# One slab of split weights converted at another place in the last attention head

## The chip, the cores and the metric

The kernel runs on one core of one Trainium2 chip. The metric is the device time of one execution in microseconds (us), the median of three runs.

The engines are named as in the profile: PE is TensorE (matmuls and transposes), DVE is VectorE, ACT is ScalarE, POOL is GpSimd, and SP is SyncE, which here only issues DMAs. Each engine works through its own instruction list in order, and an instruction waits until what it reads has been written and what it writes is free.

## The reference

The program is a diffusion backbone of two layers. Each layer projects the normed tokens (512 latent, 256 context) once, runs a convolution branch and an attention branch of eight heads on the result, merges them by gates and adds an MLP. Cut to what the change touches:

```python
for i in range(DEPTH):                                   # DEPTH = 2
    hx = modulate(rmsnorm(x, norm1_g[i]), sx1, ax1)
    px = hx @ w_in[i]                                    # [conv a | conv g | q | k | v | gates]
    q_x = apply_rope(rmsnorm(q_x, q_norm_g[i]), cos, sin)
    k_x = apply_rope(rmsnorm(k_x, k_norm_g[i]), cos, sin)
    keys = jnp.concatenate([k_x, k_c], axis=1)           # latent and context keys
    attn_x = diff_attention(q_x, keys, vals, lam, ...)   # two softmax maps a head
    # in merge_branches:
    a, g = u[..., :CONV_WIDTH], u[..., CONV_WIDTH:]      # CONV_WIDTH = 512
    z = a * jax.nn.sigmoid(g)                            # then a depthwise convolution of 31 taps
```

In the last layer the context tokens give only keys and values, no queries and no convolution.

## The kernel before

**Number format.** Every large product is computed from split fp32 operands: a high part `h`, a low part `l = x - h`, and three matmuls (lines 148 to 150): high by high, and each low part by the other's high part. A weight slab of 1024 x 256 (1 MB) is fetched by one DMA on SP's queue (line 107) into a tile with the tag `raw`, of which the attention stage has one, and then split in two halves of 128 x 1024: ACT copies the high part (`h_...`, line 76) and DVE subtracts for the low part (`l_...`, line 80). The next slab's DMA can start only when the low part of the second half is done, since it reads the raw tile. `load_slab` writes both steps; while `state["behind"]` holds instructions, the split is issued after them (`tc.issue_after`), the DMA is not.

**Attention.** Per head `h`, `qk_head(h)` projects each block of 128 tokens, norms and rotates it (ACT lines 804 and 807, DVE line 809, POOL lines 810 to 831, result `dup`) and turns it: four transposes on PE (`qkT`, line 842), a copy of the high part on ACT (line 846) and two subtractions on DVE (lines 847 and 849). `attend(h)` then makes, for each of the query blocks, the scores `S` (lines 978 and 980, two PSUM buffers), the reduction (DVE, line 982), the exponential `e` (ACT, line 985) and the difference of two softmax maps (DVE, line 995); it transposes the weights (`wT`, line 1008, into a single PSUM buffer), splits them into `wth` and `wtl` (lines 76 and 80) and multiplies them with the values (`av`). In names such as `wT0_6_1_1` the numbers are layer, head, block and half.

**Order.** A head's steps are written between those of the next head's `qk_head` (`merge`). While head 7 attends, the filling work is the projections for the convolution: `conv_a(0)`, `conv_a(1)` (blocks `ca`, slabs `wca..._0` and `wca..._1`), `conv_g(0)` and `conv_g(1)` (blocks `cg`, slabs `wcg`). Slab `a`,0 is loaded while head 7 is projected. The last two turns of head 7 are kept back (`late`) and put behind the first blocks of `conv_a(0)`: in layer 0 the two context blocks `qkT0_7_4` and `qkT0_7_5`, in layer 1 the last latent block `qkT1_7_3` and the context key (`kcD1_7`, whose norm runs over `kcT`, `rwc`, `sqe`, `rqk` and `dupc`, lines 866 to 891). `conv_a(s)` has two halves `m`; each makes a block of 512 latent tokens and, in layer 0, one of 256 context tokens. A scheduler then settles each engine's list from this program order and the waits.

**Behind.** In layer 1 DVE computes the taps of the convolution (`crun`, lines 1222 and 1226) while PE computes the merge gates (`gt`), and PE then needs their sum for a layer norm (`ln`, line 1332).

Before the change `conv_a` loads the next slab as soon as the first latent block of a slab is written, by the table `CONV_NEXT`; and `qk_head` notes a turned block in `turned` only in the last layer, at `t == 2`, so that the next head's slab is split behind it.

## Time and profile before

| | us |
|---|---|
| median of three runs | 2270.56 |
| lowest, highest | 2269.06, 2271.88 |
| profiled execution, its own time | 2273.66 |
| span of the profiled execution | 2271.9 |
| mean granted PE clock | 0.995 |

The page gives for one profiled execution the busy time of each engine in the span, and the chain of work that ended last. A row of the timeline has the start and the duration in us, the engine, the line, the instruction with its output and inputs (layer and block numbers left out), and in brackets the idle time of the engine ahead of it with what ended that. A row of the windows has the stretch, its length, the busy time (and number of instructions) of PE, of PE's weight loads, DVE, ACT and POOL, the granted clock of PE, the share of the DMA engines and GB/s.

### The profile page before, as it was taken

The numbers are of one execution on the slowest core, as the hardware profiler recorded it, in microseconds if no ns is written. First come the engines' busy times: TensorE is split into PE (matmuls) and PEld (weight loads), VectorE is DVE, ScalarE is ACT, GpSimd is POOL, SyncE is SP. The second block draws the span as 40 slices with busy tenths as digits, with TensorE's granted clock in tenths as the row PEclk, the third lists the DMA queues.
The fourth block names the chain that finished last, engine by engine and source line by source line (L and its number), as shares of the span: only waits on it lengthen the run. The fifth ranks groups of instructions, "written<-read, shape, count | busy, mean of one in ns | idle before, by whom it ended". The sixth has DMA issues, their size and how long they took to land.

```text
span 2271.9 us, 35812 instructions
## 1 busy us (share of the span) xinstructions
PE 2216.7 (98%) x14114; PEld 1999.1 (88%) x14114; DVE 1651.4 (73%) x2741; ACT 1046.9 (46%) x2035; POOL 630.9 (28%) x771
## 2 busy tenths in 40 slices
PE   7999999999999999999999999999999999999999
PEld 6999998888888999999999898999987788888887
DVE  5876777499767778788787557676759966757673
ACT  5555665432233264433445345565643333644541
POOL 1866775140000021111111345665623200000000
PEclk9999999999999999999999999999999999999999
DMA  9111102125354612332444522111114323443151
GB/s 308 57 47 47 48 27 67 45 98 169 128 174 141 203 50 65 105 121 84 139 140 144 168 75 59 45 36 52 45 61 150 115 93 121 149 135 105 57 185 38
DMA packets 202264, 232.59 MB, mean 102 GB/s; under 512 B 8864, under 2 KB 162928, under 8 KB 201968
## 3 DMA queue, kind: packets, MB, share of 16 engines
q1 hardware_dynamic: 202096, 230.30, 31.5%
q8 instruction: 111, 1.82, 0.3%
q14 instruction: 57, 0.47, 0.1%
HBM read 212.93 MB, written 17.35 MB: 101 GB/s over the span
## 4 chain that ended last, share of the span: by engine, by line
PE 75%; DVE 12%; ACT 4%; POOL 4%; DMA 3%; issue 2%; SPq 0%; DVEq 0%; POOLq 0%; ACTq 0%
PE r L157 5%; PE f L149 3%; PE f L148 3%; PE f L150 3%; PE r L148 3%; PE r L150 3%; PE r L149 3%; DVE crun L1226 3%; PE r L160 2%; PE qk L148 2%; PE qk L149 2%; PE qk L150 2%; PE gt L148 2%; PE gt L149 2%; PE gt L150 2%
## 5 line engine op out<-in xcount | busy, mean ns | idle before, releaser
L148 PE MATMUL qk<-h_wqk,h1h 128*128 128x256 f32 x640 | 182.7, 288 | 0.7 <-ACT h1h L76 0.7
L149 PE MATMUL qk<-l_wqk,h1h 128*128 128x256 f32 x640 | 180.2, 284 | 0.0
L982 DVE TENSOR_REDUCE st<-S 128x1 f32<-128x768 f32 (+1 forms) x160 | 134.4, 845 | 58.7 <-PE S L980 57.6
L150 PE MATMUL qk<-h_wqk,h1l 128*128 128x256 f32 x640 | 176.5, 284 | 0.0
L148 PE MATMUL f<-h2hh,h_w 128*128 128x512 f32 (+1 forms) x416 | 142.4, 345 | 1.5 <-ACT h2hh L76 1.4
L985 ACT ACTIVATE e<-S,st 128x768 f32<-128x768 f32 (+1 forms) x160 | 130.8, 820 | 27.9 <-DVE st L982 27.8
L149 PE MATMUL f<-h2hl,h_w 128*128 128x512 f32 (+1 forms) x416 | 143.1, 346 | 0.0
L150 PE MATMUL f<-h2hh,l_w 128*128 128x512 f32 (+1 forms) x416 | 142.5, 344 | 0.0
L148 PE MATMUL gt<-h1h,h_wg 128*128 128x512 f32 (+1 forms) x384 | 137.9, 359 | 1.0 <-ACT g L1308 1.0
L150 PE MATMUL gt<-h1h,l_wg 128*128 128x512 f32 (+1 forms) x384 | 136.1, 355 | 0.0
L149 PE MATMUL gt<-h1l,h_wg 128*128 128x512 f32 (+1 forms) x384 | 136.1, 354 | 0.0
L148 PEld LDWEIGHTS qk<-h_wqk,h1h 128*128 128x128 f32 x640 | 122.2, 191 | 3.1 <-ACT h1h L76 0.9
L157 PE MATMUL r<-F,wlor 128*128 128x512 f32 (+1 forms) x384 | 124.2, 339 | 0.4 <-DVE wlor L1639 0.4
L157 PE MATMUL r<-F,whir 128*128 128x512 f32 (+1 forms) x384 | 123.5, 337 | 0.2 <-ACT F L1582 0.2
L149 PEld LDWEIGHTS qk<-l_wqk,h1h 128*128 128x128 f32 x640 | 122.2, 191 | 0.0
L330 DVE SCALAR_TENSOR_TENSOR adaac<-ar,cvec,adaac 128x512 f32<-128x512 f32 x105 | 94.9, 926 | 35.8 <-DMA ar<-in_w_ada_dram 34.0
L150 PEld LDWEIGHTS qk<-h_wqk,h1l 128*128 128x128 f32 x640 | 119.9, 191 | 0.3 <-POOL h1l L80 0.2
L1226 DVE SCALAR_TENSOR_TENSOR cacc<-z,cols,cacc 128x783 f32<-128x783 f32 x120 | 118.8, 1045 | 0.0
L148 PE MATMUL v<-h_wv,h1h 128*128 128x256 f32 x384 | 112.3, 293 | 5.6 <-DVE qk L849 3.5
L149 PE MATMUL v<-l_wv,h1h 128*128 128x256 f32 x384 | 109.5, 285 | 0.0
L150 PE MATMUL v<-h_wv,h1l 128*128 128x256 f32 x384 | 109.4, 285 | 0.0
L810 POOL TENSOR_TENSOR rqk<-rqk,mhalf 128x4 f32<-128x4 f32 x80 | 85.8, 1075 | 76.0 <-DVE rqk L809 74.6
(406 smaller groups left out, 7392.7 us busy)
## 6 DMA issues: line engine op xcount, KB each, us to landing
r_w<-in_w_mlp_dram SPq DMA_DIRECT2D x34, 1024.0 KB, 5.3
ada<-in_w_ada_dram SPq DMA_DIRECT2D x24, 1024.0 KB, 5.3
ar<-in_w_ada_dram SPq DMA_DIRECT2D x96, 256.0 KB, 3.3
r_wg<-in_w_in_dram SPq DMA_DIRECT2D x16, 1024.0 KB, 5.4
r_wqk<-in_w_in_dram SPq DMA_DIRECT2D x30, 512.0 KB, 5.2
rf<-in_w_mlp_dram SPq DMA_DIRECT2D x26, 512.0 KB, 3.9
rr<-in_w_mlp_dram SPq DMA_DIRECT2D x24, 512.0 KB, 3.7
r_wao<-in_w_attn_out_dram SPq DMA_DIRECT2D x8, 1024.0 KB, 5.2
```

What stands on the lines that cost most here:

```text
L148: nc.tensor.matmul(ps, sh, mh, start=first, stop=False)
L149: nc.tensor.matmul(ps, sh, ml, start=False, stop=False)
L150: nc.tensor.matmul(ps, sl, mh, start=False, stop=last)
L157: nc.tensor.matmul(ps, w[j][:, k, m0 : m0 + P], a(k)[0][:, toks], start=k + j == 0, stop=False)
L160: nc.tensor.matmul(ps, w[0][:, k, m0 : m0 + P], a(k)[1][:, toks], start=False, stop=k == nk - 1)
L330: nc.vector.scalar_tensor_tensor(out=a, in0=r, scalar=cvec[:, k, q : q + 1], in1=a, op0=ALU.mult, op1=ALU.add)
L810: nc.gpsimd.tensor_tensor(out=r, in0=r, in1=mhalf[:, :4], op=ALU.pow)
L982: nc.vector.tensor_reduce(out=st[:, m : m + 1], in_=S[:, :nkey], axis=AX.X, op=ALU.max, negate=True)
L985: nc.scalar.activation(out=e[:, :nkey], in_=S[:, :nkey], func=AF.Exp, bias=st[:, m : m + 1], accum_out=st[:, 2 + m : 3 + m])
L1226: nc.vector.scalar_tensor_tensor(out=(run if t < TAPS - 1 else ca[cc])[:, :CV], in0=zt[cc][:, t : t + CV], scalar=wcol, in1=run[:, :CV], o ...
```

## The change

The slab `a`,1 is loaded in `conv_a(0)` after the second latent block, `(s, m) == (0, 1)`, in place of the first, and its split is issued behind the copies of the last head's last turned block. For that, `turned[h]` is now also set for the last head, in both layers and at every block, so that it holds the last block that is turned by then: `qkT0_7_5` in layer 0, `qkT1_7_3` in layer 1. The slab `g`,0 is loaded at the place where it was, and the table goes. No instruction is added or taken away on any engine.

```diff
-        CONV_NEXT = {("a", 0): ("a", 1), ("a", 1): ("g", 0), ("g", 0): ("g", 1)}
...
-                    if m == 0 and g is LAT:
-                        conv_w[CONV_NEXT["a", s]] = conv_load(*CONV_NEXT["a", s])
+                    if (s, m) == (1, 0) and g is LAT:
+                        conv_w["g", 0] = conv_load("g", 0)
+                    if (s, m) == (0, 1) and g is LAT:
+                        state["behind"] = turned[H - 1]
+                        conv_w["a", 1] = conv_load("a", 1)
+                        state["behind"] = ()
                     yield 5.3 if g is LAT else 2.7
...
-                if last and t == 2:
+                if last and t == 2 or h == H - 1:
                     turned[h] = hi.ins, lo.ins
```

How the engines' lists change. Behind line 740 the changed kernel's line numbers are higher by 3, so line 846 is 849 there, and 985 is 988. ACT in layer 0, from the last projection of head 7 on (`rw0_7_5`), before:

```order
L804 ACTIVATE rw0_7_5_5347<-qk0_7_5_5322 128x256
L76 ACTIVATE h_wca0_1_5444<-r_wca0_1_5442 128x1024 x2
L846 ACTIVATE qk0_7_4860<-qkT0_7_3_5361 128x4x128
L807 ACTIVATE sqe0_1_708<-rw0_7_5_5347 128x4x64
L76 ACTIVATE wth0_6_0_0_4824<-wT0_6_1_0_4991 128x3x128
L846 ACTIVATE qk0_7_4860<-qkT0_7_4_5369 128x4x128
L985 ACTIVATE e10_6_3_5168,st0_6_3_5153<-S0_6_3_1_5162,st0_6_3_5153 128x768
```

And the changed kernel on ACT, from the split of a transposed block of head 6 on, a few rows later in the list:

```order
L1026 ACTIVATE osq0_6_0_5096<-av0_6_0_5077 128x256
L1028 ACTIVATE uo0_6_0_5098<-av0_6_0_5077,ag0_141 128x256
L76 ACTIVATE wth0_6_1_0_5050<-wT0_6_2_0_5175 128x3x128
L849 ACTIVATE qk0_7_4860<-qkT0_7_5_5377 128x4x128
L76 ACTIVATE h_wca0_1_5535<-r_wca0_1_5533 128x1024 x2
L988 ACTIVATE e10_6_4_5255,st0_6_4_5244<-S0_6_4_1_5251,st0_6_4_5244 128x256
L1041 ACTIVATE rsall0_711<-av0_6_0_5077,es20_6_0_4828 128x1 x2
L76 ACTIVATE wth0_6_1_1_5052<-wT0_6_2_1_5181 128x3x128
```

The two copies `h_wca0_1` have moved from ahead of the copy of `qkT0_7_3` to behind that of `qkT0_7_5`. DVE's two subtractions `l_wca0_1` move likewise, from between two score reductions to behind its copies of `qkT0_7_5`. On SP the load of `r_wca0_1` keeps its place; `r_wcg0_0`, which needs the raw tile, moves behind the two loads of `gr` and the write of `uo0_6_0`.

ACT in layer 1, from the first copy of the slab to the copy of the last turned block, before:

```order
L76 ACTIVATE h_wca1_1_18387<-r_wca1_1_18385 128x1024
L985 ACTIVATE e11_6_3_18264,st1_6_3_18249<-S1_6_3_1_18258,st1_6_3_18249 128x768
L76 ACTIVATE h_wca1_1_18387<-r_wca1_1_18385 128x1024
L846 ACTIVATE qk1_7_17909<-qkT1_7_2_18283 128x4x128
L76 ACTIVATE wth1_6_0_1_17875<-wT1_6_1_1_18105 128x3x128
L985 ACTIVATE e01_6_3_18256,st1_6_3_18249<-S1_6_3_0_18250,st1_6_3_18249 128x768
L860 ACTIVATE kc1_7_18247<-kc1_7_18222 128x256
L868 ACTIVATE rwc1_7_18306<-kcT1_7_18303 128x256
L871 ACTIVATE sqe1_1_14387<-rwc1_7_18306 128x4x64
L846 ACTIVATE qk1_7_17909<-qkT1_7_3_18314 128x4x128
```

And the changed kernel on ACT, from the context key's copy `rwc1_7` on:

```order
L871 ACTIVATE rwc1_7_18306<-kcT1_7_18303 128x256
L849 ACTIVATE qk1_7_17909<-qkT1_7_3_18314 128x4x128
L76 ACTIVATE h_wca1_1_18442<-r_wca1_1_18440 128x1024 x2
L874 ACTIVATE sqe1_1_14387<-rwc1_7_18306 128x4x64
L1041 ACTIVATE rsall1_14390<-av1_6_0_18185,es21_6_0_17877 128x1 x2
L76 ACTIVATE wth1_6_1_1_18113<-wT1_6_2_1_18277 128x3x128
L76 ACTIVATE wth1_6_1_0_18111<-wT1_6_3_0_18291 128x3x128
L76 ACTIVATE wth1_6_1_1_18113<-wT1_6_3_1_18297 128x3x128
L894 ACTIVATE qk1_7_17909<-kcD1_7_18322 128x2x256
```

The two copies now stand behind that of `qkT1_7_3` and ahead of the context key's square `sqe1_1` and of the split `wth1_6_1_1`. On DVE the two subtractions `l_wca1_1` likewise stand behind the copies of `qkT1_7_3` and ahead of `rqk` (line 873) and `wtl1_6_1_1`.

PE in layer 1, from the transposes of a softmax block to the first block of the convolution, before:

```order
L1008 MATMUL wT1_6_2_0_18271<-cst_75,e01_6_2_18123 128x128 x3
L978 MATMUL S1_7_0_0_18335<-qk1_7_17909 128x512
L980 MATMUL S1_7_0_0_18335<-qk1_7_17909 128x512
L978 MATMUL S1_7_0_1_18343<-qk1_7_17909 128x512
L980 MATMUL S1_7_0_1_18343<-qk1_7_17909 128x512
L1034 MATMUL av1_6_0_18185<-cst_75,osq1_6_0_18204 128x1 x2
L1008 MATMUL wT1_6_2_1_18277<-cst_75,e01_6_2_18123 128x128 x3
L887 MATMUL kcD1_7_18322<-cst_75,dupc1_7_18312 128x128 x4
L148 MATMUL ca1_0_0_18359<-h1h_1_13449,h_wca1_0_18042 128x512
```

And the changed kernel on PE, from the same transposes on:

```order
L1011 MATMUL wT1_6_2_0_18271<-cst_75,e01_6_2_18123 128x128 x3
L869 MATMUL kcT1_7_18303<-cst_75,kc1_7_18247 128x128 x2
L845 MATMUL qkT1_7_3_18314<-cst_75,dup1_7_3_18177 128x128 x4
L1037 MATMUL av1_6_0_18185<-cst_75,osq1_6_0_18204 128x1 x2
L1011 MATMUL wT1_6_2_1_18277<-cst_75,e01_6_2_18123 128x128 x3
L981 MATMUL S1_7_0_0_18335<-qk1_7_17909 128x512
L983 MATMUL S1_7_0_0_18335<-qk1_7_17909 128x512
L981 MATMUL S1_7_0_1_18343<-qk1_7_17909 128x512
L983 MATMUL S1_7_0_1_18343<-qk1_7_17909 128x512
L1011 MATMUL wT1_6_3_0_18291<-cst_75,e01_6_3_18256 128x128 x3
L148 MATMUL av1_6_1_18385<-wth1_6_1_0_18111,vh1_3_17200 128x256
L1011 MATMUL wT1_6_3_1_18297<-cst_75,e01_6_3_18256 128x128 x3
```

In the list of before the transposes `wT1_6_3_0` come after 23 matmuls of `ca1_0_0`; now they stand ahead of `ca1_0_0`, with `wT1_6_3_1` and nine matmuls of `av1_6_1`. The later transposes of head 7 move forward too: `wT1_7_1_1` stood after eight matmuls of `cg1_2_0` and now stands after eight of `cg1_1_0`; `wT1_7_3_0` and `wT1_7_3_1`, which had one matmul between them, now have 33 of the merge gates and that one.

## The prediction

> **What bounds the kernel now.** I read the page first: busy shares and the chain that ended last by engine.

> ```profile
> PE 2216.7 (98%) x14114; PEld 1999.1 (88%) x14114; DVE 1651.4 (73%) x2741; ACT 1046.9 (46%) x2035; POOL 630.9 (28%) x771
> ...
> PE 75%; DVE 12%; ACT 4%; POOL 4%; DMA 3%; issue 2%; SPq 0%; DVEq 0%; POOLq 0%; ACTq 0%
> ```

> TensorE (PE) is busy for 98% of the span, so the change can only touch PE's few waits, stretches in which PE's clock is halved, and the DVE piece of the chain. Next I read the timeline of PE around both places where the second `a` slab is converted. Layer 0 (start, duration, instruction, idle time before it and what ended that):

> ```profile
> 381.73 0.44 PE L842 MATMUL qkT<-cst,dup 128*128 128x128 f32 x2 [0.20 <-POOL dup L831]
> 383.42 0.44 PE L842 MATMUL qkT<-cst,dup 128*128 128x128 f32 x2 [1.25 <-POOL dup L831]
> ...
> 385.42 0.58 PE L978 MATMUL S<-qk 128*128 128x256 f32 x1 [1.45 <-ACT e L985]
> ...
> 386.65 0.90 PE L1008 MATMUL wT<-cst,e 128*128 128x128 f32 x3 [0.43 <-DVE wtl L80]
> ...
> 390.12 0.63 PE L149 MATMUL ca<-h1l,h_wca 128*128 128x512 f32 x1
> 390.55 0.60 PE L150 MATMUL ca<-h1h,l_wca 128*128 128x512 f32 x1
> ...
> 402.48 0.50 PE L148 MATMUL ca<-h1h,h_wca 128*128 128x512 f32 x1 [0.36 <-ACT z L737]
> ...
> 415.04 0.40 PE L148 MATMUL ca<-h1h,h_wca 128*128 128x512 f32 x1
> 415.28 0.40 PE L149 MATMUL ca<-h1l,h_wca 128*128 128x512 f32 x1
> ...
> 375.00:390.00 15.00, 11.66 (x74) 10.54 (x73) 13.71 (x25) 9.74 (x20) 11.37 (x16) 0.81 0.22 70
> ```

> The waits sum to 0.20 + 1.25 + 1.45 + 0.43 + 0.36 = 3.69 us. The `ca` matmuls of 512 columns start 0.43 us apart at 390.12 but 0.24 apart at 415.04, and the granted clock of the stretch (the figure 0.81, after the busy times) is below 1: the clock is halved. A mean of 0.81 over 15 us is 0.19 x 15 / 0.5 = 5.7 us at half speed. Layer 1:

> ```profile
> 1645.34 0.52 PE L1008 MATMUL wT<-cst,e 128*128 128x128 f32 x3 [0.35 <-DVE wtl L80]
> ...
> 1648.16 0.38 PE L148 MATMUL av<-wth,vh 128*128 128x256 f32 x1 [1.34 <-ACT wth L76]
> 1649.95 0.41 PE L866 MATMUL kcT<-cst,kc 128*128 128x128 f32 x2 [1.41 <-DVE qk L849]
> 1650.89 1.11 PE L842 MATMUL qkT<-cst,dup 128*128 128x128 f32 x4 [0.54 <-DVE wtl L80]
> ...
> 1650.00:1660.00 10.00, 9.42 (x48) 8.28 (x49) 5.43 (x11) 3.98 (x10) 4.24 (x6) 0.83 0.37 120
> ```

> Here the waits sum to 3.64 us, and 0.17 x 10 / 0.5 = 3.4 us run at half speed.

> **Layer 0: what goes.** The conversions and what they hold up:

> ```profile
> 379.72 2.00 ACT L76 ACTIVATE h_wca<-r_wca 128x1024 fp32r<-128x1024 f32 x2
> ...
> 381.56 1.21 DVE L80 TENSOR_TENSOR l_wca<-r_wca,h_wca 128x1024 fp32r<-128x1024 f32 x1
> ...
> 380.94 2.42 POOL L831 TENSOR_TENSOR dup<-rw,gr 128x256 f32<-128x256 f32 x2
> 387.89 1.42 POOL L831 TENSOR_TENSOR dup<-rw,gr 128x256 f32<-128x256 f32 x2
> ```

> ACT spends 2.00 us on the high parts ahead of the copy of the head's fourth block; DVE spends 2 x 1.21 on the low parts between two score reductions; and POOL's pair that makes `dup` takes 2.42 us beside a DVE subtraction, 1.42 without. With the conversions gone from here, POOL's second half is ready 1.0 us earlier, and the exponential that frees the scores' buffer is not behind 2.0 us of ACT and 1.2 of DVE. Replaying PE's new order with these durations leaves 0.2 (first transposes), 0.6 (second), 0.5 (`wT0_6_1_1`) and 0.4 (scores, and `qkT0_7_5` behind them), and I add 0.3 for what the replay misses: 2.0 us for 3.69, a **gain of 1.7**.

> The clock: from 385.42 to 391 PE works 5.13 us (5.56 less the wait of 0.43) at 0.43 us a matmul for 0.24. Full clock saves 5.13 x (1 - 0.24/0.43) = 2.3; with 0.23, which most neighbouring starts show, 2.4. I take **2.4**. No row shows how few idle us keep the clock up. In the 3.4 us ahead of the drop PE was idle for 1.25 + some 0.5 of the next wait, about 1.75; my replay's worst stretch of that length has 1.3. So I take the clock as full, bounds 0 to 2.4. [...]

> What takes the conversions' place is later: they stand behind the copies of `qkT0_7_5`, about 390 to 394 us. Their slab is first read by `ca0_2_0`, which starts at 415.04: 20 us of cover. The raw buffer is single, so the next load moves:

> ```profile
> 384.80 0.38 SPq L107 DMA_DIRECT2D r_wcg<-in_w_in_dram  x1
> ...
> r_wg<-in_w_in_dram SPq DMA_DIRECT2D x16, 1024.0 KB, 5.4
> ...
> 415.37 1.08 ACT L76 ACTIVATE h_wcg<-r_wcg 128x1024 fp32r<-128x1024 f32 x1
> ```

> It is issued at about 394 in place of 384.80, behind two 32 KB loads and one output write on SP's queue, lands 5.4 us later (an equal slab) at 399.4, and is read at 415.37, or 411 if all is 4 us earlier: 11 us of cover. Cost 0; without that cover each us late would be one. Layer 0: **4.1**, bounds 1.7 to 4.4.

> **Layer 1: what comes.** Here the conversions move behind the copies of `qkT1_7_3` and thereby ahead of the context key's norm and of `wtl1_6_1_1`, for which PE's transposes `wT1_6_3_0` wait:

> ```profile
> 1646.19 1.05 ACT L76 ACTIVATE h_wca<-r_wca 128x1024 fp32r<-128x1024 f32 x1
> ...
> 1650.81 0.42 ACT L871 ACTIVATE sqe<-rwc 128x256 f32<-128x256 f32 x1
> ...
> 1656.11 0.49 ACT L76 ACTIVATE wth<-wT 128x384 fp32r<-128x384 f32 x1 [0.18 <-PE wT L1008]
> ...
> 1652.00 0.42 DVE L873 TENSOR_REDUCE rqk<-sqe 128x4 f32<-128x260 f32 x1
> 1652.68 0.43 DVE L847 TENSOR_TENSOR qk<-qkT,qk 128x256 fp32r<-128x256 f32 x1 [0.26 <-ACT qk L846]
> ...
> 1654.91 0.56 DVE L80 TENSOR_TENSOR wtl<-wT,wth 128x384 fp32r<-128x384 f32 x1 [0.91 <-ACT wth L76]
> ...
> 1645.93 1.20 POOL L811 TENSOR_TENSOR rw<-rw,rqk 128x256 f32<-128x256 f32 x1
> ...
> 1647.90 1.84 POOL L823 TENSOR_TENSOR rb<-rw,tS 128x128 f32<-128x128 f32 x2
> ...
> 1652.50 1.04 POOL L874 TENSOR_TENSOR rqk<-rqk,mhalf 128x4 f32<-128x4 f32 x1 [1.20 <-DVE rqk L873]
> ```

> Count from E, the end of ACT's copy of `qkT1_7_3`. DVE's two copies take 2 x 0.43, then the scores start (E + 0.9) and last 1.0. ACT's first half ends at E + 1.05; DVE's two subtractions of 1.21 end at E + 3.5, then `rqk` 0.42 and `wtl` 0.56: E + 4.5. PE, ready at E + 1.9, waits 2.6, less 0.3 in which its pipeline drains (the trace counts that as busy): **2.3**. POOL's `rqk` of 1.04, DVE's product of 0.4 and the next `wtl` keep the last pair `wT1_6_3_1` waiting for 0.9 more. Ahead of E: 0.35 as now; 0.2 for `av`; 1.1 for `dup` (POOL's chain, with about 0.6 and 0.9 saved in the two rows above where the subtractions no longer run beside it); 1.1 for the scores (transposes, 0.6 + 0.43 + 0.43, less the work between). Sum 6.0 for 3.64: PE is **2.3 later**. The half-clock stretch cost about 3.4 x 0.45 = 1.5; with waits that are longer than before I expect it again, so it cancels; bounds: gone, or twice.

> How much of this reaches the end is read behind it:

> ```profile
> 1702.48 1.52 DVE L1222 TENSOR_SCALAR crun<-z,cols 128x512 f32<-128x512 f32 x2
> ...
> 1710.00:1720.00 10.00, 10.00 (x49) 8.31 (x48) 10.00 (x16) 3.18 (x6) 1.87 (x1) 1.00 0.01 4
> ...
> 1724.86 0.38 PE L148 MATMUL av<-wth,vh 128*128 128x256 f32 x1 [0.58 <-ACT wth L76]
> 1725.79 0.55 PE L1008 MATMUL wT<-cst,e 128*128 128x128 f32 x3 [0.55 <-DVE wtl L80]
> ...
> 1812.76 1.12 PE L1332 MATMUL ln<-tot,cst 128*128 128x512 f32 x2 [2.71 <-DVE tot L1329]
> ```

> From 1702.48 on DVE runs the convolution's taps without a pause (10.00 of 10.00), and at 1812.76 PE waits 2.71 us for the last of them. So PE has 2.71 us in hand there, and the taps decide. In the new order PE does the last head's softmax transposes earlier among the convolution's gate blocks: `wT1_7_1_1` comes 24 matmuls of `cg` sooner, and DVE's first tap, queued behind the splits of those transposes, moves from 1702.48 to between 1699 and 1701. The same shift puts 22 matmuls of the merge gates (22 x 0.23 = 5 us) between `wT1_7_3_0` and its first reader, so the waits of 0.58 and 0.55 go: 1.1. PE reaches the norm 2.3 - 1.1 = 1.2 later, waits 2.71 - 1.2 = 1.5 less, and the taps, 1.5 to 3.5 earlier, allow it. Layer 1: a **gain of 1.5**, bounds -1.1 (second half-clock stretch, tail not shorter: 2.71 - 2.3 - 1.5) and +2.7 (the whole wait goes).

> **Sum.** 4.1 + 1.5 = 5.6 us. The profiled execution took 2273.66 us, so 2268.1; it stands 3.1 above the median of the runs (2270.56), so **2265.0** by the median.

> **Rivals.**
> - *Clock full in layer 1 too.* Then PE is 1.5 less late, the wait at the norm goes whole: 4.1 + 2.7 = 6.8, 2263.8. For it: a drop needs a stretch idle enough, and before only one followed. Against: 2.3 us is the longest wait of both kernels. [...]
> - *Clock still halved in layer 0* for one stretch of 3.4 us: it costs 1.5 of the 2.4. 5.6 - 1.5 = 4.1, 2266.5. For it: 1.3 idle us in a stretch is not far from 1.75.
> - *Layer 1 takes all of its part back*: the tail's waits stay and the taps start no earlier, 2.71 - 2.3 = 0.4, or down to -1.1: 4.1 - 0.35 = 3.75, 2266.8. For it: DVE's order is fixed and a later PE can hold its first tap.
> - *Slower.* The new waits behind `h_wca1_1` throw the clock to half and keep it there. Half speed costs about 0.45 us for each busy us, so the 5.6 are gone after 12.4 us (3.6 stretches) more than I assume; with four, 13.6 us, 6.1 us go: 2271.1. Slower by over 0.2% needs 10.1 / 0.45 = 22 us. Against: the longest run of halved clock here is two stretches.
> - *The load is not asked for later.* In the order of SP's queue `r_wca0_1` keeps its place between the same two output writes; only conversions move. That changes no term above.

> **How the numbers follow.** Forecast 0.38, clock full in layer 1 0.15, halved in layer 0 0.19, layer 1 takes it back 0.19, slower or something the replay misses 0.09. 0.2% of 2270.56 is 4.5 us, about what a measurement of this kernel can tell from no change. Below 2266.0: most of the forecast (0.34), all of the first rival, little of the next two (0.04): 0.53. Slower by over 0.2%: 0.06, from the last. The rest, 0.41, is within. The range: 2262.0, which is the best sum with both bounds (4.4 + 2.7 = 7.1, 2263.5) less 1.4, half the spread of the three runs (2269.06 to 2271.88); up to 2271.2, which takes in the slower rival's price.

> **What would show it.** Right: no half-speed stretch between 380 and 395 us, waits of about 2 us there, `ca0_1_0` near 398.4 for 402.48; in layer 1 one wait of over 2 us at transposes for `wtl`, the first tap at about 1700 less the gain of layer 0, and a shorter wait at `ln`. Wrong: PE idle before `cg0_0_0` for its weights, a granted clock under 0.9 in layer 0's stretch, or a wait at `ln` of 2.7 again.

## The result and the profile after

| | before | changed |
|---|---|---|
| median of 12 runs, us | 2272.39 | 2268.61 |
| lowest, highest | 2268.24, 2277.10 | 2265.84, 2271.69 |
| profiled execution, its own time | 2273.66 | 2268.69 |
| span of the profiled execution | 2271.9 | 2266.9 |

The ratio of the changed kernel to the one before is 0.998, 95% interval 0.9972 to 0.9987: 4.5 us (3.0 to 6.4) for a forecast of 5.6. In another set of 11 runs (e11 below) it was 0.9975 (0.9967 to 0.9984). The page of the changed kernel, busy time and chain:

```profile
PE 2218.0 (98%) x14114; PEld 2000.4 (88%) x14114; DVE 1652.4 (73%) x2741; ACT 1047.1 (46%) x2035; POOL 627.3 (28%) x771
...
PE 74%; DVE 12%; DMA 4%; ACT 4%; POOL 3%; issue 2%; SPq 0%; DVEq 0%; POOLq 0%; ACTq 0%
```

The page hardly changes: 5 us of 2270 are looked for in the timeline. The changed kernel's PE in layer 0, then POOL, ACT, DVE and SP at the same place, and the windows' row for the stretch:

```profile
380.69 0.44 PE L845 MATMUL qkT<-cst,dup 128*128 128x128 f32 x2 [0.21 <-POOL dup L834]
...
382.48 0.55 PE L1011 MATMUL wT<-cst,e 128*128 128x128 f32 x3 [0.66 <-DVE wtl L80]
...
384.49 0.38 PE L981 MATMUL S<-qk 128*128 128x256 f32 x1 [0.40 <-ACT e L988]
...
397.06 0.50 PE L148 MATMUL ca<-h1h,h_wca 128*128 128x512 f32 x1
...
379.90 1.42 POOL L834 TENSOR_TENSOR dup<-rw,gr 128x256 f32<-128x256 f32 x2
...
390.01 2.00 ACT L76 ACTIVATE h_wca<-r_wca 128x1024 fp32r<-128x1024 f32 x2
...
410.06 2.03 ACT L76 ACTIVATE h_wcg<-r_wcg 128x1024 fp32r<-128x1024 f32 x2
...
391.10 2.36 DVE L80 TENSOR_TENSOR l_wca<-r_wca,h_wca 128x1024 fp32r<-128x1024 f32 x2
...
393.49 0.38 SPq L107 DMA_DIRECT2D r_wcg<-in_w_in_dram  x1
...
375.00:390.00 15.00, 13.60 (x93) 11.99 (x92) 11.80 (x25) 9.37 (x22) 9.15 (x15) 1.00 0.05 14
```

Three waits are left, 1.27 us for 3.69, and the granted clock is 1.00 for 0.81. From the first transposes of `qkT0_7_4` to `ca0_1_0` it is 397.06 - 380.69 = 16.37 us, for 402.48 - 381.73 = 20.75. The conversions run from 390.01, and the load behind them, issued at 393.49, is read at 410.06; nothing waits for either. Layer 1, PE's waits, the conversions and the windows' row:

```profile
1640.39 0.52 PE L1011 MATMUL wT<-cst,e 128*128 128x128 f32 x3 [0.35 <-DVE wtl L80]
1642.56 0.39 PE L149 MATMUL av<-wtl,vh 128*128 128x256 f32 x1 [0.58 <-DVE wtl L80]
1645.02 0.65 PE L845 MATMUL qkT<-cst,dup 128*128 128x128 f32 x4 [0.69 <-POOL dup L831]
1647.35 0.47 PE L981 MATMUL S<-qk 128*128 128x512 f32 x1 [0.95 <-ACT h_wca L76]
1650.62 0.90 PE L1011 MATMUL wT<-cst,e 128*128 128x128 f32 x3 [2.11 <-DVE wtl L80]
1652.11 0.58 PE L148 MATMUL av<-wth,vh 128*128 128x256 f32 x1 [0.58 <-ACT wth L76]
...
1646.20 2.00 ACT L76 ACTIVATE h_wca<-r_wca 128x1024 fp32r<-128x1024 f32 x2
...
1647.29 2.36 DVE L80 TENSOR_TENSOR l_wca<-r_wca,h_wca 128x1024 fp32r<-128x1024 f32 x2
...
1640.00:1660.00 20.00, 14.72 (x77) 12.15 (x77) 10.56 (x19) 9.06 (x21) 8.62 (x11) 0.83 0.18 60
```

The waits sum to 5.26 us for 3.64; the longest, 2.11 us, is for the split `wtl1_6_1_1` behind the conversions. The clock's 0.83 over 20 us is 0.17 x 20 / 0.5 = 6.8 us at half speed (0.50 from 1649.51 to 1656.33), for 3.4 before. Behind it, the first tap, PE's waits up to the layer norm, and then the first matmul of the layer's output projection in the kernel before (first row) and in the changed one (second):

```profile
1694.72 0.81 DVE L1225 TENSOR_SCALAR crun<-z,cols 128x512 f32<-128x512 f32 x1
...
1725.87 0.61 PE L1037 MATMUL av<-cst,osq 128*128 128x1 f32 x4 [0.90 <-ACT uo L1028]
...
1759.63 0.50 PE L148 MATMUL gt<-h1h,h_wg 128*128 128x512 f32 x1 [0.24 <-ACT g L1311]
...
1798.76 0.47 PE L148 MATMUL ya<-h1h,h_wao 128*128 128x512 f32 x1 [0.76 <-ACT g L1311]
...
1805.69 1.12 PE L1335 MATMUL ln<-tot,cst 128*128 128x512 f32 x2 [0.77 <-DVE tot L1332]
```

```profile
1879.90 0.39 PE L148 MATMUL o<-mh,h_wo 128*128 128x512 f32 x1
```

```profile
1873.74 0.39 PE L148 MATMUL o<-mh,h_wo 128*128 128x512 f32 x1
```

From the first row of layer 1 (1645.34 before) to this one it is 234.56 us before and 233.35 after. So by the traces layer 0 gains 4.4 us and layer 1 1.2. The rest of the span differs between two profiles by some us either way (from that `o` to the last matmul 387.6 us before and 388.8 after; there the clock of the changed kernel was at 0.50 from 1925.99 to 1929.40 us, that of before at 1.00 throughout).

### The profile page after: what moved, and what is told of

Same layout as the page of the kernel before. It is cut to its first block, busy times and chain, and to the rows that moved or that the text cites. A ratio compares the mean times of both kernels' runs of the same rounds, so it can differ in the third digit from the quotient of the medians.

```text
span 2266.9 us, 35816 instructions
## 1 busy us (share of the span) xinstructions
PE 2218.0 (98%) x14114; PEld 2000.4 (88%) x14114; DVE 1652.4 (73%) x2741; ACT 1047.1 (46%) x2035; POOL 627.3 (28%) x771
## 4 chain that ended last, share of the span: by engine, by line
PE 74%; DVE 12%; DMA 4%; ACT 4%; POOL 3%; issue 2%; SPq 0%; DVEq 0%; POOLq 0%; ACTq 0%
PE r L157 4%; PE f L149 4%; PE f L150 4%; PE f L148 3%; PE r L148 3%; PE r L149 3%; PE r L150 3%; PE qk L148 3%; DMA ar<-in_w_ada_dram 2%; PE qk L149 2%; PE qk L150 2%; DVE crun L1229 2%; PE gt L148 2%; PE gt L149 2%; PE gt L150 2%
## 5 line engine op out<-in xcount | busy, mean ns | idle before, releaser
L148 PE MATMUL qk<-h_wqk,h1h 128*128 128x256 f32 x640 | 182.6, 287 | 0.7 <-ACT h1h L76 0.7
L149 PE MATMUL qk<-l_wqk,h1h 128*128 128x256 f32 x640 | 180.2, 284 | 0.0
L985 DVE TENSOR_REDUCE st<-S 128x1 f32<-128x768 f32 (+1 forms) x160 | 134.4, 846 | 59.3 <-PE S L983 58.3
L150 PE MATMUL qk<-h_wqk,h1l 128*128 128x256 f32 x640 | 176.5, 284 | 0.0
L148 PE MATMUL f<-h2hh,h_w 128*128 128x512 f32 (+1 forms) x416 | 142.9, 347 | 1.5 <-ACT h2hh L76 1.4
L149 PE MATMUL f<-h2hl,h_w 128*128 128x512 f32 (+1 forms) x416 | 143.9, 347 | 0.0
L150 PE MATMUL f<-h2hh,l_w 128*128 128x512 f32 (+1 forms) x416 | 143.3, 346 | 0.0
L148 PE MATMUL gt<-h1h,h_wg 128*128 128x512 f32 (+1 forms) x384 | 137.9, 359 | 0.2 <-ACT g L1311 0.2
L149 PE MATMUL gt<-h1l,h_wg 128*128 128x512 f32 (+1 forms) x384 | 136.1, 354 | 0.0
L150 PE MATMUL gt<-h1h,l_wg 128*128 128x512 f32 (+1 forms) x384 | 136.0, 354 | 0.0
L148 PEld LDWEIGHTS qk<-h_wqk,h1h 128*128 128x128 f32 x640 | 122.2, 191 | 2.9 <-ACT h1h L76 0.9
L149 PEld LDWEIGHTS qk<-l_wqk,h1h 128*128 128x128 f32 x640 | 122.2, 191 | 0.1
L150 PEld LDWEIGHTS qk<-h_wqk,h1l 128*128 128x128 f32 x640 | 119.9, 191 | 0.3 <-POOL h1l L80 0.2
L148 PE MATMUL v<-h_wv,h1h 128*128 128x256 f32 x384 | 113.1, 294 | 5.6 <-DVE qk L852 3.5
L149 PE MATMUL v<-l_wv,h1h 128*128 128x256 f32 x384 | 110.3, 287 | 0.0
L150 PE MATMUL v<-h_wv,h1l 128*128 128x256 f32 x384 | 110.0, 286 | 0.0
## 6 DMA issues: line engine op xcount, KB each, us to landing
r_w<-in_w_mlp_dram SPq DMA_DIRECT2D x34, 1024.0 KB, 5.3
ada<-in_w_ada_dram SPq DMA_DIRECT2D x24, 1024.0 KB, 5.5
r_wg<-in_w_in_dram SPq DMA_DIRECT2D x16, 1024.0 KB, 5.3
r_wao<-in_w_attn_out_dram SPq DMA_DIRECT2D x8, 1024.0 KB, 5.3
```

Source lines behind the costliest of these rows:

```text
L148: nc.tensor.matmul(ps, sh, mh, start=first, stop=False)
L149: nc.tensor.matmul(ps, sh, ml, start=False, stop=False)
L150: nc.tensor.matmul(ps, sl, mh, start=False, stop=last)
L985: nc.vector.tensor_reduce(out=st[:, m : m + 1], in_=S[:, :nkey], axis=AX.X, op=ALU.max, negate=True)
```

## The experiments

All runs on one table. The stretch of layer 0 goes from the first transposes of `qkT0_7_4` to the first matmul of `cg0_0_0`, that of layer 1 from the transposes `wT1_6_1_1` (1645.34 before) to the first `o` (1879.90), both read from PE's timeline of the one profile of each run. The ratios are to the runs of the kernel before in the same set. The columns say where the conversions stand. The rest of a list need not be that of before, since the scheduler settles the whole program anew: in e1 and e7 the lists of PE, DVE and ACT differ from before's in layer 1 too, from some 1650 us on; in e5 only from 1810 us on (in all three also in a few rows at layer 1's start, 1350 to 1370 us), and in e3 nowhere.

| run | layer 0 | layer 1 | ratio, interval | layer 0, us | layer 1, us |
|---|---|---|---|---|---|
| before | before | before | | 57.19 | 234.56 |
| change | moved | moved | 0.998 (0.9972 to 0.9987) | 52.72 | 233.35 |
| e1 | moved | before | 0.9995 (0.9987 to 1.0004) | 52.73 | 234.76 |
| e2 | before | moved | 0.9995 (0.9986 to 1.0004) | 56.28 | 233.33 |
| e3 | before | before | 1.0005 (0.9996 to 1.0014) | 57.66 | 233.88 |
| e4 | moved | behind the context key | 0.9964 (0.9951 to 0.9976) | 52.69 | 227.31 |
| e5 | low parts alone moved | before | 0.9997 (0.9988 to 1.0007) | 54.17 | 236.19 |
| e6 | before | behind the context key | 0.9972 (0.9961 to 0.9982) | 57.67 | 228.65 |
| e7 | moved | before | 0.9996 (0.9987 to 1.0004) | 52.73 | 237.06 |
| e8 | moved, split twice | moved | 0.9974 (0.9964 to 0.9984) | 52.71 | 233.41 |
| e9 | moved | behind the context key | 0.9962 (0.9950 to 0.9975) | 52.71 | 227.44 |
| e10 | before | behind the context key | 0.9974 (0.9965 to 0.9983) | 57.24 | 228.64 |
| e11 | moved | moved | 0.9975 (0.9967 to 0.9984) | 52.69 | 232.49 |
| e12 | before | moved | 0.9993 (0.9985 to 1.0002) | 57.60 | 233.49 |

**Layer 0 alone (e1, and again e7).** The condition picks the layer:

```diff
+                    if last and (s, m) == (0, 0) and g is LAT:
+                        conv_w["a", 1] = conv_load("a", 1)
-                    if (s, m) == (0, 1) and g is LAT:
+                    if not last and (s, m) == (0, 1) and g is LAT:
```

> Only layer 0's conversions move; layer 1 stays as before. Theory of the prediction: most of the gain is here, 4.4 us in the profile of the changed kernel (ca0_1_0 starts 16.4 us after the first transposes of qkT0_7_4, for 20.75 before), so the ratio is about 0.998 (4 us), with PE's waits in the stretch about 1.3 us and the granted clock 1.00 there; layer 1 waits 3.6 us at the late turn and 2.7 at ln. Rival one, that the half-clock stretch of before was chance and not due to these waits: then only the waits count, 1.7 to 2.4 us (0.999). Rival two, that layer 0's gain is caught again by a later wait: 0.9995 or more, and a longer wait somewhere between 400 and 640 us.

> The kernel of the first run once more, since its time (0.9995, interval 0.9987 to 1.0004) is below what its trace shows for layer 0 (16.4 us for 20.75, 4.4 gained) and its profile had a wait of 1.56 us and a half-clock stretch at 971 us that no other profile has. Theory: the first sample was unlucky; ratio 0.998 to 0.9985 and no wait near 971. Rival, that the earlier layer 0 makes that wait regularly: 0.9995 again, and the wait is there again.

In both traces layer 0 is 4.5 us shorter, as in the change, and its waits are the same three. The time is only about one us shorter: 0.9995 and 0.9996, with intervals that end at 3.0 us. So the first sample was not unlucky. The wait of 1.56 us near 971 is not regular either: e7 does not have it, but e9 has. In e9's trace:

```profile
972.66 0.38 PE L157 MATMUL r<-F,whir 128*128 128x256 f32 x1 [1.56 <-ACT F L1730]
```

What both have in common is a dearer layer 1, though its conversions stand as before. One part is the clock. The windows over the late turn, e7 and then e3, whose lists are alike up to there:

```profile
1635.00:1655.00 20.00, 16.17 (x83) 13.59 (x82) 11.44 (x20) 8.94 (x19) 9.12 (x11) 0.83 0.18 60
```

```profile
1640.00:1660.00 20.00, 16.24 (x99) 14.27 (x99) 14.10 (x24) 10.49 (x25) 9.83 (x15) 0.91 0.18 60
```

That is 6.8 us at half speed for 3.6. e1 and e5, whose conversions in layer 1 stand as before too and which shorten layer 0, also show 0.83 over such 20 us; the profile of before shows 0.91 like e3. The other part is the list behind the late turn, which is another one. In e7 the stretch of layer 1 begins with the first row here, and the first tap, the second row, comes 59.0 us later (58.4 in e1), for 57.1 in before and in e3 and 57.6 in e5, which lost as much clock with before's list:

```profile
1637.40 0.52 PE L1013 MATMUL wT<-cst,e 128*128 128x128 f32 x3 [0.35 <-DVE wtl L80]
...
1696.39 1.52 DVE L1227 TENSOR_SCALAR crun<-z,cols 128x512 f32<-128x512 f32 x2
```

Together they make the stretch of layer 1 235.9 us (mean of e1 and e7) for 234.2 (before and e3): 1.7 of the 4.5 us are lost there, and the 2.8 that remain lie just inside each of the two intervals. The granted clock is known of every run: its mean is 0.9951 and 0.9946 over the runs of e1 and e7, and 0.9945 to 0.9950 over the three sets of before. So about as much time ran at half speed with layer 0 moved as without: what the clock gained in layer 0 it lost elsewhere.

**Layer 1 alone (e2, and again e12).** The same with the condition turned round.

> Only layer 1's conversions move. Theory of the prediction: 1.5 us gain (2.1 in the profile of the changed kernel up to ln), ratio 0.9991 to 0.9995; waits at the late turn sum to about 5 us with one of 2.1 us for wtl, and the wait at ln falls from 2.7 us to about 0.8. Rival, that layer 1 gives back what its longer waits cost: ratio 1.000 to 1.001 and ln waits as before.

> Layer 0 as before, layer 1 behind qkT1_7_3 (the second run again). By theory A 0.9993 to 1.000; by theory B 0.9990 to 0.9995.

0.9995 and 0.9993, 1.1 and 1.6 us, and the trace as expected: waits of 5.3 us with one of 2.10, and 0.75 and 0.79 at `ln`. Both rows of the table are about 1 us under those of before and e3. The rival, that layer 1 gives back all it gains, is not borne out by the traces; the intervals of the times alone would allow it.

**The place without the dependence (e3).**

```diff
                     if (s, m) == (0, 1) and g is LAT:
-                        state["behind"] = turned[H - 1]
                         conv_w["a", 1] = conv_load("a", 1)
-                        state["behind"] = ()
```

> The slab is loaded at the new place in the program but not issued behind the turned block. The engines' lists are then the same as before's, instruction for instruction. Theory: ratio 1.000 (0.9993 to 1.0007); the place does nothing, the dependence does all. Rival, that the place moves the request on the DMA queue: 0.998 like the change. As a second profile of the lists of before it also shows whether the half-clock stretch at layer 0's late turns comes again.

All five engines' lists come out the same as before's, and the time is the same within its interval. So "asked for later" has no part in the result: the scheduler pulls the conversions forward again, and only the dependence on the turned block holds them. The half-clock stretch of layer 0 comes again:

```profile
380.00:400.00 20.00, 16.66 (x88) 14.27 (x87) 12.79 (x25) 9.16 (x20) 8.83 (x12) 0.83 0.20 63
```

It was there in all six profiles with layer 0 as before (before, e2, e3, e6, e10, e12), and in none of the seven with it moved.

**Behind the context key in layer 1 (e4, and again e9).** The conversions wait for the copies of `ctx_turn`, and the slab is loaded where `conv_a(1)` begins:

```diff
+            if last and s:
+                state["behind"] = turned[H - 1]
+                conv_w["a", 1] = conv_load("a", 1)
+                state["behind"] = ()
...
+                if h == H - 1:                 # in ctx_turn, behind its two copies
+                    turned[h] = hi.ins, lo.ins
```

> As the change in layer 0; in layer 1 the conversions wait for the copies of the context key's turn, one step later than in the change, so they no longer stand ahead of the context key's norm and of wtl1_6_1_1. Theory: the wait of 2.1 us for that split goes and the waits at the late turn fall from 4.7 us (0.58, 0.69, 0.95, 2.11, 0.58, less what comes anew) to about 3; the taps then bind, so the gain over the change is 0.8 us or less at ln, ratio 0.9975 to 0.998. Rival, that conversions beside ca1_0_0 delay the scores of head 7 or the slab for ca1_2_0: same as the change or slower, 0.998 to 0.9995.

> One of four kernels that make a square: layer 0 moved or not, by layer 1 as in the change or behind the context key's turn. This one: layer 0 moved, layer 1 behind the context key (the fourth run again). Open is why layer 0 alone measures 1.0 us where its traces show 4.4 at ca0_1_0. Theory A: the gain is there in every run, and is lost later where layer 1's list of before halves the clock for longer (two stretches of 3.41 us for one in the traces); with the list of layer 1 that shows no half clock, layer 0 is then worth about 4 us: this kernel 4 us faster than the next one, ratio 0.996 to 0.997. Theory B: runs without a profile halve the clock in layer 0 less often than the profiled ones, so only the waits count, 1.7 us: 1.5 to 2 us between the two.

This is the fastest of all: 0.9964 and 0.9962, 8.2 and 8.6 us under before. PE's waits at the late turn in e4's trace, with the windows' row:

```profile
1640.72 0.52 PE L1017 MATMUL wT<-cst,e 128*128 128x128 f32 x3 [0.36 <-DVE wtl L80]
1642.89 0.39 PE L149 MATMUL av<-wtl,vh 128*128 128x256 f32 x1 [0.58 <-DVE wtl L80]
1645.35 0.66 PE L849 MATMUL qkT<-cst,dup 128*128 128x128 f32 x4 [0.69 <-POOL dup L835]
1647.68 0.47 PE L987 MATMUL S<-qk 128*128 128x512 f32 x1 [0.95 <-ACT wth L76]
1649.77 0.39 PE L148 MATMUL av<-wth,vh 128*128 128x256 f32 x1 [0.58 <-ACT wth L76]
1650.36 0.55 PE L1017 MATMUL wT<-cst,e 128*128 128x128 f32 x3 [0.21 <-DVE wtl L80]
...
1640.00:1660.00 20.00, 16.63 (x104) 13.93 (x103) 12.70 (x22) 10.63 (x24) 8.17 (x11) 1.00 0.15 49
```

The wait of 2.11 us is gone, the others stand, one of 0.21 is new, and the clock stays full. I had expected at most 0.8 us over the change, since the taps would bind; layer 1 became 6 us shorter, and `ln` no longer waits at all. That bound was wrong: the taps begin earlier when PE's blocks ahead of them do (in e4 the first one 50.1 us behind the first row, in the change 54.3), so the wait at `ln` was no floor.

**The same in layer 1 with layer 0 as before (e6, and again e10).**

> Layer 0 as before, layer 1 with the conversions behind the context key's turn as in the fourth run. If the parts add, the fourth run's gain of 0.36% (8 us) is 4.3 us from layer 0 and the rest from layer 1: ratio 0.9984 (0.998 to 0.9988), and the interval from the layer norm of layer 0's MLP to the convolution's output of layer 1 is 7 us shorter than before's 536. Rival, that the fourth run was lucky in its layer 1: 0.9995.

> Layer 0 as before, layer 1 behind the context key (the sixth run again). By theory A 0.998 to 0.9985 and 4 us over the kernel ahead; by theory B about 0.9972 again and 1.5 to 2 us over it.

0.9972 and 0.9974, where I had expected 0.9984 of e6: layer 1 in this form is worth 6 us by itself, more than the change as a whole.

**Only the low parts late in layer 0 (e5).** In layer 0, DVE's subtractions alone are issued behind the turned block; ACT's copies go where they were.

```diff
-                        state["behind"] = turned[H - 1]
+                        which = "behind" if last else "lows"
+                        held = state[which]
+                        state[which] = () if last else turned[H - 1][1]
                         conv_w["a", 1] = conv_load("a", 1)
-                        state["behind"] = ()
+                        state[which] = held
```

> In layer 0 ACT's two high parts stay where they were before, ahead of the copy of qkT0_7_3, and only DVE's two low parts wait behind the copies of qkT0_7_5; layer 1 as before. It tells apart what of the slab's split held PE up. Theory A, DVE's subtractions (they block POOL's dup and the score reductions): PE's second wait for dup falls from 1.25 us to about 0.1, the scores' wait from 1.45 to 0.5 or less, no half clock, so ca0_1_0 comes 17 us after the first transposes of qkT0_7_4. Theory B, ACT's 2.00 us ahead of the exponential: the scores' wait stays at 1.2 us or more and the clock is halved again, 19 to 20.5 us. Time by either: 0.998 to 0.9995.

PE's waits in e5, with the windows' row:

```profile
381.37 0.44 PE L847 MATMUL qkT<-cst,dup 128*128 128x128 f32 x2 [0.21 <-POOL dup L836]
382.05 0.44 PE L847 MATMUL qkT<-cst,dup 128*128 128x128 f32 x2 [0.25 <-POOL dup L836]
...
384.06 0.58 PE L983 MATMUL S<-qk 128*128 128x256 f32 x1 [1.10 <-ACT e L990]
...
380.00:400.00 20.00, 18.35 (x110) 16.18 (x109) 13.81 (x29) 10.80 (x27) 7.65 (x15) 0.91 0.19 60
```

Each theory is right for one wait. DVE's subtractions were what held POOL's `dup` (1.25 to 0.25); ACT's copies hold the exponential (1.10 of 1.45 stays). The clock is halved for about 3.6 us, and the stretch is 54.17 us, 3.1 under the mean of 57.27 of the six with layer 0 as before, 1.5 over the full change. The time, 0.9997, does not tell the theories apart; its layer 1 ran at half speed for 6.8 us, as in e1 and e7.

**The split written twice in layer 0 (e8).** The cover is loaded with 2.0 us more on ACT and 2.4 more on DVE:

```diff
-                split(hi[:, k], lo[:, k], rs[n], eng)
+                for _ in range(state["times"]):        # 2 in layer 0, 1 elsewhere
+                    split(hi[:, k], lo[:, k], rs[n], eng)
```

> As the change, but in layer 0 the slab's high and low parts are written twice at the new place, 2.0 us more on ACT and 2.4 more on DVE. It prices the cover that I cost at 20 us. Theory: the work is hidden; ca0_1_0 comes 16.4 to 16.8 us after the first transposes and no new wait of PE over 0.3 us stands before cg0_0_0. Rival, that the place is tight: a wait of 1 to 2 us at the softmax transposes of head 6 or at ca0_2_0.

ACT's four copies in two pairs, then all of PE's waits up to 440 us:

```profile
391.24 2.00 ACT L76 ACTIVATE h_wca<-r_wca 128x1024 fp32r<-128x1024 f32 x2
394.70 2.04 ACT L76 ACTIVATE h_wca<-r_wca 128x1024 fp32r<-128x1024 f32 x2
...
381.94 0.44 PE L848 MATMUL qkT<-cst,dup 128*128 128x128 f32 x2 [0.21 <-POOL dup L837]
383.73 0.55 PE L1014 MATMUL wT<-cst,e 128*128 128x128 f32 x3 [0.66 <-DVE wtl L80]
385.74 0.39 PE L984 MATMUL S<-qk 128*128 128x256 f32 x1 [0.39 <-ACT e L991]
```

The waits are those of the change, none is added: the new place is well covered.

**The change again (e11), and the square.**

> The change itself once more: layer 0 moved, layer 1 behind qkT1_7_3. 0.998 (0.997 to 0.9987) by both theories; by theory A 3 to 4 us under the next kernel, by theory B 1.5 to 2.

Moving layer 0 is worth 3.4 and 4.1 us where layer 1 is moved (0.998 against 0.9995, 0.9975 against 0.9993), 1.8 and 2.7 where layer 1 stands behind the context key (0.9964 against 0.9972, 0.9962 against 0.9974), and 1.0 where it is as before. Each of these differences has some 2 us on either side. Theory A fits the first pair; the second is nearer to theory B's 1.5 to 2. Theory B fails on the traces, since all six profiles with layer 0 as before lose the clock there, but it was about runs that leave no trace. That layer 0's gain is in part lost again in layer 1 fits the three profiles with the longer half-clock stretch, e1, e5 and e7. It points to the clock that e5, with before's list up to 1810 us, has as long a layer 1 (236.2) as e1 and e7 (235.9), though their first tap is later; but no run here has the whole of layer 0 moved and before's list, unchanged, behind it, so how much the other list takes is not settled.

## Why the prediction was right

**Layer 0, waits.** Forecast 2.0 us left of 3.69, measured 1.27. The second wait for `dup` went whole where the replay left 0.6; `wT0_6_1_1` (0.5 forecast, 0.66) and the scores (0.4, 0.40) came as replayed. POOL's pair went from 2.42 to 1.42 us, as the quoted row away from the slab's subtractions said, and e5, where these alone moved, has PE's second wait for `dup` at 0.25 us for 1.25. The pair took 1.0 us longer beside a subtraction of 1.21 us; another pair of before took 2.43 us (at 108.21), beside the subtraction `l_wqk` of 1.22 us. Not every subtraction did this: the pair of 1.42 us at 387.89 ran beside the `wtl` of 0.56 us at 388.11. Why it takes longer there is not shown.

**Layer 0, clock.** Forecast full, worth 2.4; it was full in all seven profiles with layer 0 moved. The whole term, 4.1, measured 4.6 at `cg0_0_0` (57.27, the mean of six, less 52.71, that of seven): 2.4 from the waits, for 1.7, and so about 2.1 from the clock, for 2.4. e3 rules out the rival that the drop of before was chance.

**The cover.** Forecast 394 for the next load and 411 for its reader: 393.49 and 410.06. e8 put 4.4 us more behind the same place for nothing. The rival that the load is not asked for later was right, and e3 shows it cost nothing.

**Layer 1.** The sum was near (1.5 forecast; about 1.0 by the mean of before and e3, 234.2, less that of the five moved, 233.2; 1.7 with e5 among those of before; 1.1 and 1.6 by the times of e2 and e12), but in part by luck, with terms that erred against each other:
- The waits came to 5.26, not 6.0; the one for `wtl1_6_1_1`, counted from E as 2.3, was 2.11. No run shows the 0.3 us taken off there for the draining of PE's pipeline: by the rows a `ca` matmul counts as busy for 0.40 us where the next starts 0.24 behind it, 0.16 more.
- The clock was to cost the same as before. It was halved for 6.8 us in four of five profiles of this list (3.4 in e11): the mis-sized term, some 1.5 us, inside its stated bounds.
- In the tail three waits went (0.58, 0.55 and 0.82: 1.95 us), not two (1.1).
- The forecast's sum takes the whole wait at `ln` (2.71 - 2.3 + 1.1 = 1.5), though its words have it 1.5 less. The wait fell by 1.94, to 0.77. Before it, one of 0.76 is new, and that for `gt`, 0.98 in the profile of before but 0.26 in e3, is 0.24.
- Four matmuls that stood ahead of `ln` now stand behind it, about 0.9 us. So `ln` starts 2.1 us earlier in the stretch, but `o` only 1.2.
- The first tap moved by 1702.48 - 1694.72 = 7.8 us, of which 1645.34 - 1640.39 = 5.0 came from upstream: 2.8, in the forecast range of 1.5 to 3.5.

**The sum.** 5.6 forecast; 4.5 and 5.7 measured. The time itself, 2268.61 for 2265.0, is further off, since the kernel before also measured 2272.39 for the 2270.56 that the forecast started from. What the prediction did not see is that the parts need not simply add: moving layer 0's conversions gives layer 1 another list and other half-speed stretches, and in e1 and e7 only about one of layer 0's four us arrives.

**The rival of the clock in layer 1** named the larger prize without seeing how to get it: with the conversions one step later (e4, e9) the long wait and the halving both go, and the kernel is 8 us faster than before.

## What to carry to other kernels

When work is moved off a critical stretch, count what stands next in the in-order lists behind its new place: here the conversions left one wait and made another of 2.11 us in layer 1, and one step further they made none of that size. In a scheduled kernel, a later line in the program may move nothing; compare the engines' lists before believing that it did, and compare them over the whole program: an edit for one layer changed the order in the other. And a few short waits close together cost more than their sum when the clock is lost with them: in layer 0, 2.4 us of waits went and the stretch became 4.6 us shorter.

## What the runs showed of the hardware

The clock of PE fell after waits much shorter than the stretch that it then stayed low: in layer 0 those of before were at most 1.45 us. Where it fell, it stayed at half for about 3.4 or 6.8 us: in before from 384.17 to 391.00, from 1401.34 to 1404.76 and from 1650.52 to 1653.93 us, with a granted clock of 0.50. These stretches also begin whole multiples of 3.413 us apart: 1017.17 and 249.18 us are 298 and 73 of them. So do those of the changed kernel, at 1366.20, 1396.92, 1649.51 and 1925.99 us, 9, 74 and 81 of them apart.

```profile
1647.11:1650.52 3.41, 0.79 (x3) 0.39 (x3) 3.17 (x5) 2.28 (x7) 3.26 (x5) 1.00 0.09 16
1650.52:1653.93 3.41, 3.04 (x14) 3.04 (x15) 3.07 (x7) 1.46 (x4) 1.73 (x4) 0.50 0.86 291
```

```profile
1639.18:1642.59 3.41, 1.72 (x14) 1.41 (x12) 2.64 (x4) 3.41 (x7) 3.26 (x4) 1.00 0.00 0
1642.59:1646.00 3.41, 1.83 (x8) 1.18 (x8) 3.30 (x7) 1.79 (x5) 2.86 (x5) 0.50 0.41 118
```

```profile
1642.77:1646.18 3.41, 2.60 (x21) 2.37 (x22) 2.46 (x5) 1.70 (x6) 2.75 (x5) 1.00 0.11 38
1646.18:1649.60 3.41, 2.05 (x12) 1.29 (x11) 2.26 (x5) 1.81 (x6) 1.74 (x2) 1.00 0.00 1
```

In before the four waits fall mostly into one piece, idle for 2.62 us; PE works through most of the next, and one stretch is lost. In e1 the same waits fall half into each of two pieces, idle for 1.69 and 1.58, and two are lost. In e4 no piece is idle for more than 1.36, and the clock stays full, as in the four profiles with that list. So one list does not always lose the same: layer 1's list of before, alike in its waits here in five profiles, lost 3.4 us in two and 6.8 in three, and the change's 6.8 in four and 3.4 in one. (e7's second stretch does not fit: its piece is idle for only 0.20. Where the clock comes back is not settled.) A reading of one profile can thus be off by one such stretch, about 1.5 us (3.41 x (1 - 0.24/0.43)), at each place where PE waits.
